# A hybrid encoder trunk on one core: the last product and its norm in two parts of 256 tokens, and another order of the sums and scalings ahead of the MLP

## The chip, the cores and the metric

The kernel runs on one core of a Trainium2 chip. The metric is the device time of one execution in microseconds; the median of three runs is given.

The engines are named as in the profile: PE is TensorE (PEld its weight loads), DVE is VectorE, ACT is ScalarE, POOL is GpSimd, SP is SyncE, which here only issues transfers. Each engine works through its own queue in the order in which the program issued the instructions to it; an instruction whose operand is not there holds up everything behind it in that queue.

## The reference, cut to what matters

One layer of an encoder on 1024 tokens of 1024 channels, all float32. Four token mixers make `merged`; then

```python
x = x + g1 * (merged @ w_out)
h2 = rmsnorm(x, norm2_g) * (1.0 + sc2) + sh2
f = square(relu(h2 @ w_ff1)) @ w_ff2          # D_FF = 4096
x = x + g2 * f
return rmsnorm(x, final_g)
```

with `rmsnorm(x, g) = x * rsqrt(mean(x*x over channels) + eps) * g`. The change touches only these lines: the second norm, the MLP's sums of weights, and the last product with the final norm.

## The kernel before

**Layout.** Tokens lie along the free dimension, channels on the partitions. `xg[k][t]` holds x for one half k of the channel blocks (even or odd) and one half t of the tokens (512 each): four slices m of 128 channels by 512 tokens. `xb(k, t, m)` is one slice.

**Precision.** A float32 product is made of three fp32r products: each operand is split into a high part (`whi`, `xhi`: a ScalarE copy) and a low part (`wlo`, `xlo`: VectorE subtracts), and TensorE adds up hi·hi, hi·lo and lo·hi.

**Stages and granules.** The second half of the program (`phase2`) is a list of 128 granules. Stage 0 is the product with `w_out` (granules 0 to 15). Stages 1 to 8 are the MLP: `w_ff1` and `w_ff2` in four blocks, each product by a scheme of seven instead of eight smaller products, so each stage has seven positions of two granules (h = 0, 1). Stage s begins at granule 16 + 14(s-1). The scheme needs sums of quarter matrices first: S1 to S4 of the weights, T1 to T4 of the other operand, all made by VectorE in pieces of 128x1024 (`wr<-wr,wr` in the profile for the weights). A granule is 24 matmuls of 512 columns (two halves p, four banks m, three products c), about 5.4 us. The two granules of a position fill four PSUM banks; the positions alternate between two sets of banks (`pm` and `pb` in the profile). `take` (or `take_out` in stage 0) reads a finished set: VectorE adds it into x, and where a norm follows, `square` squares x on ScalarE and VectorE adds the squares into `acc[t]`.

**The order by hand.** Iteration G of the loop issues, in this order: the taking of the last set, the matmuls of granule G with the functions of `at[(G, "mid")]` between their halves and those of `at[(G, "end")]` behind them, loads of weights, sums of weights (`w2_add`) for the granules ahead, sums of the other operand (`x2_add`), the weight split of granule G + 3 (`w2_split`), operand splits (`x2_split`), more loads. `w2_add(J)` makes the sums that granule J needs, as far as their forms are loaded and no form that is still to be split would be overwritten; what is missing is tried again later. It looks up to G + 4, and up to G + 8 for 8 <= G < 20.

**The norms.** `columns(t, bank)` adds the last squares, transposes `acc[t]` by TensorE in four blocks, reduces, takes the inverse root and makes `diag`, a diagonal block matrix; `spread(bank)` multiplies it with ones, so that every partition has the row, and ScalarE copies it to `rb`. `normed` then scales (VectorE) and shifts (ScalarE) x for the MLP; `final` scales x by the final gain and `rb` on VectorE and stores each slice of 256 KB, by SP and ACT in turn. For t = 1 the second norm's columns stand in the middle of granule 17, its spread in the middle of 18, and `normed` at the end of 18. The final norm of t = 0 has its columns in the middle of granule 125, its spread in the middle of 126, its scalings at the ends of 126 and 127. Behind the loop the last set (k = 0, t = 1) is taken, and t = 1 is normed and stored.

Of the kernel before, what the change touches and what calls it, by code (L numbers as in the profile page):

```python
# [6 lines left out]
F32 = mybir.dt.float32  # L7
F32R = mybir.dt.float32r
I32 = mybir.dt.int32
ACTF = mybir.ActivationFunctionType  # L10
ALU = mybir.AluOpType
# [33 lines left out]
class Program:  # L45
# [1502 lines left out]
    def phase2(self):  # L1548
        I, const, work = self.I, self.const, self.work
        md = {}  # L1550
# [14 lines left out]
        xg = self.xg = [[tile(f"xg{k}{t}", [128, 4, 512]) for t in range(2)] for k in range(2)]  # L1565
# [8 lines left out]
        xout = self.out.rearrange("(m k) p (t n) -> k t p m n", k=2, t=2)  # L1574
        for k, t in ((0, 0), (1, 0), (1, 1), (0, 1)):
            self.G.dma_start(out=xg[k][t], in_=xin[k, t])
        banks = [[self.mps() for _ in range(4)], [self.bps() for _ in range(4)]]
        xb = lambda k, t, m: xg[k][t][:, m, :]
        fb = lambda k, t, m: self.fr[k][t][m // 2][:, m % 2, :]
        ub = lambda m: self.u[m // 2][:, m % 2, :]  # L1580
        acc = [self.nrm[0][:, t, :] for t in range(2)]
        sqs = [self.nrm[1][:, t, :] for t in range(2)]
        diag, rb = (self.nrm[2][:, t, :] for t in range(2))
        begun = set()
# [6 lines left out]
        def take_out(i):  # L1591

            k, t = ((0, 0), (1, 0), (1, 1), (0, 1))[i]
            for m in range(4):
                upd(0, k, t, m, banks[i % 2][m])
                square(t, k, m)
            self.G.dma_start(out=xsp[k][t], in_=xg[k][t].rearrange("p c n -> p (c n)"))
# [51 lines left out]


        nsq, late = [0], []
        def square(t, k, m):

            if t not in begun:
                begun.add(t)
                self.act(acc[t], xb(k, t, m), ACTF.Square)
                return
            sq = sqs[nsq[0] % 2]
            nsq[0] += 1
            self.act(sq, xb(k, t, m), ACTF.Square)  # L1660
            squares()
            late.append((acc[t], sq))

        def squares():
            while late:
                a, sq = late.pop()
                self.add(a, a, sq)

        def columns(t, bank):

            squares()
            ss = self.sm.tile([128, 4], F32, tag="ss", name=self.name("ss"))
            for b in range(4):
                self.tr(bank[:, b * 128:(b + 1) * 128], acc[t][:, b * 128:(b + 1) * 128])
            self.reduce(ss, bank.rearrange("p (b c) -> p b c", c=128))
            r = self.drain(self.gen_rsqrt(ss, D))
            self.tt(diag.rearrange("p (b q) -> p b q", q=128), self.ident.unsqueeze(1).to_broadcast([128, 4, 128]),
                    r.unsqueeze(2).to_broadcast([128, 4, 128]), ALU.mult)
            begun.discard(t)

        def spread(bank):
            self.mm(bank, self.ones, diag)
            self.act(rb, bank, ACTF.Copy)

        def normed(k, t, h):
            for m in (2 * h, 2 * h + 1):
                d, x = 2 * m + k, xb(k, t, m)
                self.stt(x, x, A2[:, d:d + 1], rb, ALU.mult, ALU.mult)
                self.act(x, x, ACTF.Identity, bias=B2[:, d:d + 1])

        def final(k, t, h):
            for m in (2 * h, 2 * h + 1):
                d, x = 2 * m + k, xb(k, t, m)
                self.stt(x, x, self.col("fg", d), rb, ALU.mult, ALU.mult)
                self.dma(xout[k, t][:, m, :], x, "SA"[m % 2])

        at = {}
        on = lambda G, place, f: at.setdefault((G, place), []).append(f)
# [3 lines left out]
            on(10 + h, "end", lambda h=h: (normed(0, 0, h), normed(1, 0, h)))  # L1702
        on(17, "mid", lambda: columns(1, banks[1][0]))
        on(18, "mid", lambda: spread(banks[0][0]))
        for h in range(2):
            on(18, "end", lambda h=h: (normed(1, 1, h), self.x2_split(20 + h)))
        for h in range(2):
            on(18, "end", lambda h=h: (normed(0, 1, h), self.x2_add(22 + h)))
        on(27, "end", lambda: [self.dma(xg[k][t].rearrange("p c n -> p (c n)"), xsp[k][t]) for k, t in ((0, 0), (1, 1), (1, 0), (0, 1))])
        e = self.first(8)  # L1710
        on(e + 11, "mid", lambda: columns(0, banks[1][0]))
        on(e + 12, "mid", lambda: spread(banks[0][0]))
        for h in range(2):
            on(e + 12 + h, "end", lambda h=h: (final(0, 0, h), final(1, 0, h)))


        n_g = len(self.gran)
        for G in range(-4, n_g):
            if G >= 0:
                s, pos, h = self.gran[G]  # L1720
                if s == 0:
                    if G and G % 4 == 0:
                        take_out(G // 4 - 1)
                    bank, begins, ends, skip = banks[G // 4 % 2], G % 4 == 0, G % 4 == 3, False
                else:
                    n, (kind, order) = 7 * (s - 1) + pos, self.STAGES[s]
                    if h == 0:
                        take(n - 1) if n else take_out(3)
                    i, bank = order[pos], banks[n % 2]
                    skip = pos > 1 and order[pos - 2] == self.GOES_ON[kind].get(i)  # L1730
                    begins, ends = h == 0 and not skip, h == 1
                (whi, wlo), (xhi, xlo) = self.wops[G % 4], self.xop[G % 4]
                for p in range(2):
                    if p:
                        for f in at.get((G, "mid"), ()):
                            f()
                    for m in range(4):
                        o = slice(p * 512 + m * 128, p * 512 + (m + 1) * 128)
                        for c, (w, x) in enumerate(((whi, xhi), (whi, xlo), (wlo, xhi))):
                            self.mm(bank[m], w[:, o], x[:, p, :], start=begins and p == c == 0,  # L1740
                                    stop=ends and p == 1 and c == 2, skip=skip)
                for f in at.get((G, "end"), ()):
                    f()
            self.w2_loads(G + 8)
            for J in range(G + 1, min(G + (9 if 8 <= G < 20 else 5), n_g)):
                if 0 <= J:
                    self.w2_add(J)
            for J in range(G + 1, min(G + 5, n_g)):
                if J >= 0 and self.x2_own(J) and not 20 <= J < 24 and self.x2_there(J) <= G:
                    self.x2_add(J)  # L1750
            if G >= -3:
                self.w2_split(G + 3)
            for J in range(G + 1, min(G + 4, n_g)):
                if J >= 0 and self.x2_own(J) and (not 20 <= J < 24 or G >= 19) and self.x2_there(J) <= G:
                    self.x2_split(J)
            if G >= -3:
                self.x2_load(G + 3)
            self.w2_loads(G + 8)
        take(7 * 7 + 6)
        columns(1, banks[0][1])  # L1760
        spread(banks[0][2])
        for h in range(2):
            final(1, 1, h)
            final(0, 1, h)


def pack(inp):
# [67 lines left out]
```

## Time and profile before

| | |
|---|---|
| median of three runs | 1682.4 us (1679.68 to 1684.09) |
| profiled execution | 1681.92 us, span 1680.1 us, mean granted TensorE clock 0.991 |
| TensorE matmul busy | 1630.0 us (97%) |
| VectorE busy | 1259.2 us (75%) |
| ScalarE busy | 664.8 us (40%) |
| GpSimd busy | 64.9 us (4%) |

The span runs from the first to the last instruction of the profiled execution; the time of that execution is 1.8 us longer. Busy times are sums over the whole span, and matmul records overlap, so a busy TensorE is not one at its peak. Where an instruction waited, its row says in brackets how long its engine was idle ahead of it and which instruction ended that.

### The profile page before, as it was taken

The numbers are of one execution on the slowest core, as the hardware profiler recorded it, in microseconds if no ns is written. First come the engines' busy times: TensorE is split into PE (matmuls) and PEld (weight loads), VectorE is DVE, ScalarE is ACT, GpSimd is POOL, SyncE is SP. The second block draws the span as 40 slices with busy tenths as digits, with TensorE's granted clock in tenths as the row PEclk, the third lists the DMA queues.
The fourth block names the chain that finished last, engine by engine and source line by source line (L and its number), as shares of the span: only waits on it lengthen the run. The fifth ranks groups of instructions, "written<-read, shape, count | busy, mean of one in ns | idle before, by whom it ended". The sixth has DMA issues, their size and how long they took to land.

```text
span 1680.1 us, 19346 instructions
## 1 busy us (share of the span) xinstructions
PE 1630.0 (97%) x7390; PEld 1341.3 (80%) x7390; DVE 1259.2 (75%) x1906; ACT 664.8 (40%) x864; POOL 64.9 (4%) x126
## 2 busy tenths in 40 slices
PE   6999999999999999999999999899999999999995
PEld 4888878888878888888888888687888888888883
DVE  8889787779877865455666658899549947984897
ACT  5433323554336536541221335643243334323442
POOL 0000000000000000000000001100110010012000
PEclk9999999999999999999999999999999999999997
DMA  8522425533545453054564725661671274157102
GB/s 314 177 84 65 133 103 151 177 137 114 165 142 194 164 175 137 26 188 150 188 238 163 274 81 195 225 231 46 211 272 31 100 251 177 44 175 262 58 1 100
DMA packets 83679, 257.03 MB, mean 153 GB/s; under 512 B 9857, under 2 KB 22273, under 8 KB 82562
## 3 DMA queue, kind: packets, MB, share of 16 engines
q1 hardware_dynamic: 61186, 174.00, 30.6%
q0 software_dynamic: 17792, 67.12, 10.8%
q10 hardware_dynamic: 4608, 14.68, 2.2%
q8 instruction: 58, 0.95, 0.2%
q14 instruction: 35, 0.29, 0.1%
HBM read 199.14 MB, written 54.53 MB: 151 GB/s over the span
## 4 chain that ended last, share of the span: by engine, by line
PE 79%; DVE 14%; issue 2%; DMA 2%; ACT 2%; SPq 0%; DVEq 0%; ACTq 0%
PE pm L91 56%; PE pb L91 22%; DVE xg L122 2%; DVE wlo L105 2%; DVE xlo L105 1%; DVE fr L105 1%; DVE wr L105 1%; DVE t L105 1%; DVE s L126 1%; DVE fr L122 1%; DMA ada<-ada 1%; DVE nrm L105 1%; PE pb L96 1%; DVE ssacc L105 0%; DVE v L105 0%
## 5 line engine op out<-in xcount | busy, mean ns | idle before, releaser
L91 PE MATMUL pm<-act,whi 128*128 128x512 f32 x2176 | 672.9, 391 | 1.8 <-ACT act L146 1.6
L91 PEld LDWEIGHTS pm<-act,whi 128*128 128x128 f32 x2176 | 405.6, 188 | 88.3 <-ACT act L146 3.6
L91 PE MATMUL pm<-act,wlo 128*128 128x512 f32 x1088 | 419.8, 389 | 0.0
L146 ACT ACTIVATE whi<-wr 128x1024 fp32r<-128x1024 f32 x124 | 130.9, 1057 | 313.7 <-PE pm L91 133.0
L91 PEld LDWEIGHTS pm<-act,wlo 128*128 128x128 f32 x1088 | 204.3, 188 | 42.8
L105 DVE TENSOR_TENSOR wlo<-wr,whi 128x1024 fp32r<-128x1024 f32 x124 | 151.3, 1221 | 113.3 <-ACT whi L146 113.3
L91 PE MATMUL pm<-xhi,whi 128*128 128x512 f32 x512 | 201.0, 393 | 4.2 <-ACT whi L146 4.2
L91 PE MATMUL pb<-xhi,whi 128*128 128x512 f32 x512 | 201.0, 393 | 2.4 <-DVE xg L122 2.3
L91 PE MATMUL pm<-xhi,wlo 128*128 128x512 f32 x512 | 200.4, 391 | 2.0 <-DVE wlo L105 2.0
L91 PE MATMUL pm<-xlo,whi 128*128 128x512 f32 x512 | 200.1, 391 | 0.0
L91 PE MATMUL pb<-xhi,wlo 128*128 128x512 f32 x512 | 199.8, 390 | 0.0
L91 PE MATMUL pb<-xlo,whi 128*128 128x512 f32 x512 | 199.8, 390 | 0.0
L146 ACT ACTIVATE whi<-wraw 128x1024 fp32r<-128x1024 f32 x74 | 78.1, 1057 | 104.1 <-PE pm L91 87.4
L91 PEld LDWEIGHTS pm<-xhi,whi 128*128 128x128 f32 x512 | 96.7, 189 | 24.8 <-ACT whi L146 4.6
L91 PEld LDWEIGHTS pb<-xhi,whi 128*128 128x128 f32 x512 | 96.4, 188 | 24.1 <-ACT whi L146 2.7
L91 PEld LDWEIGHTS pm<-xhi,wlo 128*128 128x128 f32 x512 | 96.7, 189 | 22.6 <-DVE wlo L105 2.4
L91 PEld LDWEIGHTS pm<-xlo,whi 128*128 128x128 f32 x512 | 96.7, 189 | 20.5 <-DVE xlo L105 0.3
L91 PEld LDWEIGHTS pb<-xlo,whi 128*128 128x128 f32 x512 | 96.6, 189 | 20.3 <-issue 0.5
L91 PEld LDWEIGHTS pb<-xhi,wlo 128*128 128x128 f32 x512 | 96.5, 189 | 20.2
L105 DVE TENSOR_TENSOR wlo<-wraw,whi 128x1024 fp32r<-128x1024 f32 x74 | 90.1, 1219 | 8.0 <-ACT whi L146 7.7
L105 DVE TENSOR_TENSOR wr<-wr,wr 128x1024 f32<-128x1024 f32 x64 | 78.0, 1221 | 0.8
L105 DVE TENSOR_TENSOR xlo<-fr,xhi 128x1024 fp32r<-128x1024 f32 x54 | 65.9, 1220 | 11.7 <-ACT xhi L146 11.7
(263 smaller groups left out, 1879.8 us busy)
## 6 DMA issues: line engine op xcount, KB each, us to landing
wr<-w SPq DMA_DIRECT2D x76, 512.0 KB, 4.7
ada<-ada SPq DMA_DIRECT2D x48, 512.0 KB, 6.3
xhi<-hop POOLq DMA_DIRECT2D x42, 512.0 KB, 3.6
xlo<-hop POOLq DMA_DIRECT2D x42, 512.0 KB, 4.7
wraw<-wgate SPq DMA_DIRECT2D x32, 512.0 KB, 3.9
tg<-tg ACTq DMA_DIRECT2D x24, 512.0 KB, 2.8
tl<-tg SPq DMA_DIRECT2D x24, 512.0 KB, 5.6
wraw<-win SPq DMA_DIRECT2D x20, 512.0 KB, 3.6
```

Source lines behind the costliest of these rows:

```text
L91: self.P.matmul(out=out, lhsT=lhsT, rhs=rhs, start=start, stop=stop, skip_group_check=skip)
L96: self.P.transpose(out, a, self.ident)
L105: self.V.tensor_tensor(out=out, in0=a, in1=b, op=op)
L122: self.V.scalar_tensor_tensor(out=out, in0=a, scalar=s, in1=b, op0=op0, op1=op1, **kw)
L126: self.V.tensor_tensor_scan(out=out, data0=a, data1=b, initial=0.0, op0=ALU.mult, op1=ALU.add)
L146: self.A.activation(out=out, in_=a, func=f, **kw)
```

## The change

- The look-ahead of `w2_add` is split in two for all G: sums for granules up to G + 4 where they stood, and sums for G + 5 to G + 8 at the end of the iteration, behind the splits.
- The block at the end of granule 18 is issued in another order: both halves of `normed(1, 1)` first, then an operand split, one half of `normed(0, 1)`, another split, the other half, and the sums of granules 22 and 23 last.
- The loop ends at granule 125. The last product (granules 126 and 127) is made in two parts of 256 tokens, one after the other, each of 48 matmuls of 256 columns; the first part goes to the low halves of one set of banks, the second to the other set. The first part is taken while the second is multiplied, and its columns stand ahead of the second part's last 12 matmuls.
- Each part has its own columns and spread of 256 tokens. `last` scales a slice of 256 tokens by the final gain and directly by the spread bank, without a copy to `rb`, and stores it (128 KB) by SP or ACT. Between the two spreads stand two products of ones whose results are not used.
- For t = 0 the gain is multiplied in on ScalarE (`scaled`, eight copies with a scale at the end of granule 125) and `rb` on GpSimd (`final`, four products of 128x1024), stored in four transfers of 512 KB by SP.

```diff
-        def square(t, k, m):
+        def square(t, k, m, cut=slice(0, 512)):
+            a, x = acc[t][:, cut], xb(k, t, m)[:, cut]
...
-        def columns(t, bank):
+        def columns(t, bank, cut=slice(0, 512)):
             squares()
-            for b in range(4):
-                self.tr(bank[:, b * 128:(b + 1) * 128], acc[t][:, b * 128:(b + 1) * 128])
-            self.reduce(ss, bank.rearrange("p (b c) -> p b c", c=128))
+            a, d, nb = acc[t][:, cut], diag[:, cut], (cut.stop - cut.start) // 128
+            for b in range(nb):
+                self.tr(bank[:, b * 128:(b + 1) * 128], a[:, b * 128:(b + 1) * 128])
+            self.reduce(ss, bank[:, 0:128 * nb].rearrange("p (b c) -> p b c", c=128))
...
+        def spread(bank, cut=None):
+            if cut is None:
+                self.mm(bank, self.ones, diag)
+                self.act(rb, bank, ACTF.Copy)
+            else:
+                self.mm(bank[:, 0:cut.stop - cut.start], self.ones, diag[:, cut])
...
-        def final(k, t, h):
-            for m in (2 * h, 2 * h + 1):
-                d, x = 2 * m + k, xb(k, t, m)
-                self.stt(x, x, self.col("fg", d), rb, ALU.mult, ALU.mult)
-                self.dma(xout[k, t][:, m, :], x, "SA"[m % 2])
+        def scaled(k, t):
+            for m in range(4):
+                self.act(xb(k, t, m), xb(k, t, m), ACTF.Copy, scale=self.col("fg", 2 * m + k))
+
+        def final(k, t):
+            for h in range(2):
+                x = xg[k][t][:, 2 * h:2 * h + 2, :]
+                self.G.tensor_tensor(out=x, in0=x, in1=rb.unsqueeze(1).to_broadcast([128, 2, 512]), op=ALU.mult)
+                self.dma(xout[k, t][:, 2 * h:2 * h + 2, :], x)
+
+        def last(k, m, bank, cut):
+            x, d = xb(k, 1, m)[:, cut], 2 * m + k
+            self.stt(x, x, self.col("fg", d), bank[:, 0:cut.stop - cut.start], ALU.mult, ALU.mult)
+            self.dma(xout[k, 1][:, m, cut], x, "SA"[m % 2])
...
-        for h in range(2):
-            on(18, "end", lambda h=h: (normed(1, 1, h), self.x2_split(20 + h)))
-        for h in range(2):
-            on(18, "end", lambda h=h: (normed(0, 1, h), self.x2_add(22 + h)))
+        on(18, "end", lambda: (normed(1, 1, 0), normed(1, 1, 1), self.x2_split(20), normed(0, 1, 0), self.x2_split(21),
+                               normed(0, 1, 1), self.x2_add(22), self.x2_add(23)))
...
-        for h in range(2):
-            on(e + 12 + h, "end", lambda h=h: (final(0, 0, h), final(1, 0, h)))
+        on(e + 11, "end", lambda: (scaled(1, 0), scaled(0, 0)))
...
-        for G in range(-4, n_g):
+        for G in range(-4, n_g - 2):
...
-            for J in range(G + 1, min(G + (9 if 8 <= G < 20 else 5), n_g)):
-                if 0 <= J:
-                    self.w2_add(J)
+            for J in range(max(G + 1, 0), min(G + 5, n_g)):
+                self.w2_add(J)
...
             self.w2_loads(G + 8)
-        take(7 * 7 + 6)
-        columns(1, banks[0][1])
-        spread(banks[0][2])
-        for h in range(2):
-            final(1, 1, h)
-            final(0, 1, h)
+            for J in range(max(G + 5, 0), min(G + 9, n_g)):
+                self.w2_add(J)
+
+        take(7 * 7 + 5)
+        cuts = (slice(0, 256), slice(256, 512))
+        low, high = slice(0, 256), slice(256, 512)
+
+        def take_part(q):
+            for m in range(4):
+                x, d = xb(0, 1, m)[:, cuts[q]], 2 * m
+                self.stt(x, banks[1 - q][m][:, low], md["g2"][:, d:d + 1], x, ALU.mult, ALU.add)
+                square(1, 0, m, cuts[q])
+
+        def finals(q, bank):
+            for m in range(4):
+                for k in range(2):
+                    yield last(k, m, bank, cuts[q])
+
+        for q in range(2):
+            for h in range(2):
+                (whi, wlo), (xhi, xlo) = (o[(n_g - 2 + h) % 4] for o in (self.wops, self.xop))
+                for p in range(2):
+                    if (q, h, p) == (1, 1, 1):
+                        columns(1, banks[1][2][:, high], cuts[0])
+                    for m in range(4):
+                        o = slice(p * 512 + m * 128, p * 512 + (m + 1) * 128)
+                        for c, (w, x) in enumerate(((whi, xhi), (whi, xlo), (wlo, xhi))):
+                            self.mm(banks[1 - q][m][:, low], w[:, o], x[:, p, cuts[q]], start=h == p == c == 0,
+                                    stop=h == p == 1 and c == 2)
+                    if (q, h, p) == (0, 0, 0):
+                        spread(banks[0][0])
+                        final(1, 0)
+                        final(0, 0)
+            take_part(q)
+        spread(banks[1][3][:, high], cuts[0])
+        for _ in range(2):
+            self.mm(banks[1][0], self.ones, acc[0])
+        first, second = finals(0, banks[1][3][:, high]), finals(1, banks[0][1][:, high])
+        for _ in range(3):
+            next(first)
+        columns(1, banks[0][0][:, high], cuts[1])
+        spread(banks[0][1][:, high], cuts[1])
+        for _ in first:
+            pass
+        for _ in second:
+            pass
```

## Rows read from the trace of the kernel before

**Rows 1.** The page's first line.
```profile
span 1680.1 us, 19346 instructions
```

**Rows 2.** Windows: us from:to, length, busy PE, PEld, DVE, ACT, POOL, clock, DMA.
```profile
1012.00:1038.00 26.00, 26.00 (x116) 21.35 (x114) 25.58 (x30) 13.73 (x17) 4.79 (x10) 1.00 0.62 243
...
1058.00:1066.00 8.00, 1.86 (x8) 0.92 (x6) 7.14 (x8) 4.22 (x5) 0.53 (x1) 0.88 0.04 18
1066.00:1138.00 72.00, 72.00 (x307) 59.19 (x308) 68.39 (x76) 36.57 (x45) 7.94 (x15) 0.97 0.65 241
...
1146.00:1576.00 430.00, 429.87 (x1895) 355.37 (x1895) 313.98 (x338) 153.85 (x178) 44.07 (x84) 1.00 0.46 158
```

**Rows 3.** Chain that ended last: start us, us, engine, output, line, count.
```profile
1064.57 1.23 DVE wlo L105
1065.84 7.60 PE pm L91 x22
1073.45 10.88 PE pb L91 x48
...
1141.17 12.77 PE pb L91 x48
```

**Rows 4.** Timeline of PE: start us, us; in brackets idle before and its releaser.
```profile
249.60 0.61 PE L91 MATMUL pb<-v,ca 128*128 128x128 f32 x4
250.05 0.39 PE L91 MATMUL pb<-u,intra 128*128 128x128 f32 x2
...
1038.35 0.66 PE L96 MATMUL pb<-ident,nrm 128*128 128x128 f32 x4 [0.17 <-DVE nrm L105]
...
1141.17 0.47 PE L91 MATMUL pb<-xhi,whi 128*128 128x512 f32 x1 [2.31 <-DVE xg L122]
...
1657.84 0.39 PE L91 MATMUL pb<-xhi,wlo 128*128 128x512 f32 x1
```

**Rows 5.** Timeline of DVE, granules 12 to 18.
```profile
1015.99 2.47 DVE L105 TENSOR_TENSOR wr<-wr,wr 128x1024 f32<-128x1024 f32 x2
...
1033.06 2.36 DVE L105 TENSOR_TENSOR wr<-wr,wr 128x1024 f32<-128x1024 f32 x2
...
1037.60 0.69 DVE L105 TENSOR_TENSOR nrm<-nrm,nrm 128x512 f32<-128x512 f32 x1
...
1041.83 3.61 DVE L105 TENSOR_TENSOR wr<-wr,wr 128x1024 f32<-128x1024 f32 x3
...
1046.49 1.41 DVE L122 SCALAR_TENSOR_TENSOR xg<-xg,A,nrm 128x512 f32<-128x512 f32 x2
```

**Rows 6.** Timeline of ACT: high weight parts, and rb copied from its bank.
```profile
1016.11 1.99 ACT L146 ACTIVATE whi<-wr 128x1024 fp32r<-128x1024 f32 x2
...
1033.18 1.05 ACT L146 ACTIVATE whi<-wr 128x1024 fp32r<-128x1024 f32 x1
...
1045.36 0.60 ACT L146 ACTIVATE nrm<-pm 128x512 f32<-128x512 f32 x1 [2.29 <-PE pm L91]
...
1652.44 0.58 ACT L146 ACTIVATE nrm<-pm 128x512 f32<-128x512 f32 x1
```

**Rows 7.** Timeline of DVE, the block behind granule 18 and granule 32's taking.
```profile
1049.79 1.23 DVE L105 TENSOR_TENSOR xlo<-xg,xhi 128x1024 fp32r<-128x1024 f32 x1 [1.89 <-ACT xhi L146]
...
1057.57 1.23 DVE L105 TENSOR_TENSOR xg<-xg,xg 128x1024 f32<-128x1024 f32 x1 [0.79 <-ACT xg L146]
...
1140.28 2.72 DVE L122 SCALAR_TENSOR_TENSOR xg<-pb,g,xg 128x512 f32<-128x512 f32 x4
```

**Rows 8.** Timeline of DVE behind the last matmul.
```profile
1658.36 0.75 DVE L122 SCALAR_TENSOR_TENSOR xg<-pb,g,xg 128x512 f32<-128x512 f32 x1
...
1665.54 0.69 DVE L130 TENSOR_REDUCE ss<-pm 128x4 f32<-128x512 f32 x1 [1.21 <-PE pm L96]
...
1667.71 0.69 DVE L105 TENSOR_TENSOR nrm<-ident,rsq 128x512 f32<-128x512 f32 x1
...
1671.20 5.39 DVE L122 SCALAR_TENSOR_TENSOR xg<-xg,cols,nrm 128x512 f32<-128x512 f32 x8 [2.80 <-ACT nrm L146]
```

**Rows 9.** Groups by line and shape, DVE: count, busy us, mean ns, idle before.
```profile
L105 DVE TENSOR_TENSOR tt<-tt,t 128x256 f32<-128x256 f32 x16 | 6.1, 422 | 0.3
```

More of the change, by code (lines that the diff above doesn't have):

```diff
@@ L1651, in phase2 @@
         nsq, late = [0], []
-        def square(t, k, m):
+        def square(t, k, m, cut=slice(0, 512)):
+            a, x = acc[t][:, cut], xb(k, t, m)[:, cut]
             if t not in begun:
                 begun.add(t)
-                self.act(acc[t], xb(k, t, m), ACTF.Square)
+                self.act(a, x, ACTF.Square)
                 return
-            sq = sqs[nsq[0] % 2]
+            sq = sqs[nsq[0] % 2][:, cut]
             nsq[0] += 1
-            self.act(sq, xb(k, t, m), ACTF.Square)
+            self.act(sq, x, ACTF.Square)
             squares()
-            late.append((acc[t], sq))
+            late.append((a, sq))
         def squares():
@@ L1667, in squares @@
                 self.add(a, a, sq)
-        def columns(t, bank):
+        def columns(t, bank, cut=slice(0, 512)):
             squares()
-            ss = self.sm.tile([128, 4], F32, tag="ss", name=self.name("ss"))
-            for b in range(4):
-                self.tr(bank[:, b * 128:(b + 1) * 128], acc[t][:, b * 128:(b + 1) * 128])
-            self.reduce(ss, bank.rearrange("p (b c) -> p b c", c=128))
-            r = self.drain(self.gen_rsqrt(ss, D))
[L1677 to L1683, printed above, removed]
+            a, d, nb = acc[t][:, cut], diag[:, cut], (cut.stop - cut.start) // 128
+            ss = self.sm.tile([128, 4], F32, tag="ss", name=self.name("ss"))[:, 0:nb]
+            for b in range(nb):
+                self.tr(bank[:, b * 128:(b + 1) * 128], a[:, b * 128:(b + 1) * 128])
+            self.reduce(ss, bank[:, 0:128 * nb].rearrange("p (b c) -> p b c", c=128))
+            r = self.drain(self.gen_rsqrt(ss, D))
+            self.tt(d.rearrange("p (b q) -> p b q", q=128), self.ident.unsqueeze(1).to_broadcast([128, nb, 128]),
+                    r.unsqueeze(2).to_broadcast([128, nb, 128]), ALU.mult)
+            if cut.stop == 512:
+                begun.discard(t)
+        def spread(bank, cut=None):
[4 more added lines that the diff above has]
+                self.mm(bank[:, 0:cut.stop - cut.start], self.ones, diag[:, cut])
         def normed(k, t, h):
```

## The prediction, made before the changed kernel had run

> **What bounds the kernel now.** I read the windows first, for where each engine is full, then the chain that ended last, then the queues of TensorE, VectorE and ScalarE around the two places that the change touches. The span is 1680.1 us [rows 1]. From granule 34 on (1146 us) TensorE is full to the end of the products and VectorE has air: 429.9 of 430 us against 314 [rows 2]. So work moved between engines there costs and gives nothing; a gain must come from a place where TensorE waits. Three count; a short wait ahead of columns(0) in granule 125 keeps the same work ahead of it.
>
> At the start of stage 1 VectorE is the bound: 25.6 of 26 us busy up to 1038, 68.4 of 72 between 1066 and 1138 [rows 2]. TensorE pauses in granule 21 until 1065.84, when its low weight part has been split [rows 3], and again before granule 34, 2.31 us, because the bank that it is to write has not been taken [rows 4]. Behind the first pause the granted clock fell to the lower of its two levels, 1.2 GHz: 0.88 is the mean of that window [rows 2], and the 22 matmuls behind it took 7.60 us where 48 take 10.88, so 2.6 us more than at full clock. Behind the second, 48 took 12.77, 1.9 more [rows 3].
>
> The third place is the tail. The last matmul starts at 1657.84 and ends at 1658.2 [rows 4], and what follows runs in a line: taking the bank and adding squares from 1658.36, transposes, the reduction at 1665.54, root and diagonal at 1667.71, the spread, eight scalings from 1671.20 to 1676.59, and 3.5 us for the last transfer and the closing wait [rows 8].
>
> **The order of the weight sums.** The three sums S2, S4, S3 of granule 21 take 3.5 us on VectorE from 1041.83, and the split behind them 1.1 more, up to the first scaling at 1046.49; today they are issued in iteration 17, behind the norm's columns, so they fill the time in which diag goes through TensorE and comes back as rb [rows 5, 6]. By the new rule the sums of granule J+5 and beyond stand at the end of an iteration. S4 overwrites a form that iteration 16 has split by then, so all three are issued at the end of iteration 16: ahead of columns(1), not behind it. Following the queue:
>
> In iteration 12 the split of granule 15 now stands ahead of S1 and S2 of granule 20. VectorE is free at 1015.99, the high part ends at 1016.11 + 1.04, so VectorE idles 1.15 us where it had a sum to do [rows 5, 6]; some 0.3 of small gaps further on take that up: +0.9. In iteration 16 the split of granule 19 follows the bank's taking (which ends at 1033.06) at once, and its high part, at 1033.18, needs 1.05: +1.2 [rows 5, 6]. The last add of squares, at 1037.60 today, so starts 3.5 + 0.9 + 1.2 = 5.6 later. TensorE, which waits 0.17 ahead of the transposes today [rows 4], waits 5.6 more.
>
> From the transposes to the end of the copy of rb it is 1038.35 to 1045.96, 7.6 us, of which TensorE's 24 matmuls and the spread are most [rows 4, 6]. VectorE has the diagonal ready 3.5 us after the transposes start, at 1041.83, and then only the split of granule 20, 1.1 us. It idles 7.6 - 3.5 - 1.1 = 3.0 us.
>
> The new order of the norm gives some back. Four scalings now run in one go, and the waits for ScalarE fall from two of 1.9 and two of 0.8 us to two of 1.9 [rows 7]: with an overlap at the end I take 1.7 off. Sum on VectorE up to the split of granule 21, today at 1064.57 [rows 3]: 0.9 + 1.2 + 3.0 - 1.7 = +3.4 us. From there VectorE runs full to the taking at 1140.28 [rows 7], which lets granule 34 start, and the six sums of granules 32 to 35 stand ahead of it in either order, so nothing is won back on that way; TensorE's time is set by VectorE again.
>
> To this comes the clock. The new pause of 5.6 us is nearly as long as TensorE's idle 6.1 us in the window from 1058 to 1066, in which it fell [rows 2]. The 24 matmuls and the spread behind the transposes are on the path, and at the lower level they lose between nothing and the 2.6 us measured there. I take 2.2. **Stage 1: +5.6 us, between +3.4 and +6.0.** The sums of the later stages move four granules ahead inside iterations where TensorE never waits; their loads stand granules ahead of them, and VectorE has 116 us of air there: nothing.
>
> **The last product in two parts.** 96 matmuls of 256 columns replace 48 of 512, which take 10.88 us [rows 3]. The trace has none of that width. Below, half of 0.227 us, and no loss; above, the full 0.227 us each, 10.9 us more, if something fixed set the pace. The nearest row is four records of 128 columns, each with a weight load of its own, that start within 0.45 us, counted to the next row [rows 4]: a load fits in 0.113 us, so I take 0.12 and +0.6 us. Two pauses come in: the spread writes a bank that is being taken (0.4), and the second part's first bank is the one that ScalarE copies rb from, a copy that ends at 1653.0 today [rows 6] and about 0.6 later behind the eight new copies with a scale (half of the 1.04 us for 1024 elements each) [rows 6]. TensorE ends 1.6 us later, at 1659.8.
>
> On VectorE a 256-wide add is 0.42 us alone [rows 9], about 0.34 one behind another, and 0.40 with a PSUM source (half of the eight in 5.39 us [rows 8], with the fixed part). The eight scalings of the other token half leave it for GpSimd; they ran while TensorE was busy, so their going is worth only that the first part's taking finds VectorE free. Its transposes stand 12 matmuls ahead of TensorE's end, at 1658.2; 0.5 us to the reduction, 1.9 from there to the diagonal (2.17 today [rows 8] less the shorter reduction) and 0.4 for it make 1661.0, when VectorE can start on part two: 2.6 us of taking and adds, 1.2 for three scalings, 0.4 for the last add, and 0.5, 1.9 and 0.4 again: 1668.0. Five scalings cover the spread, at either clock, and eight follow it, 5.2 us in all: 1673.2. With the same 3.5 us behind it the span ends at 1676.7. **Tail: -3.4 us, between -1.5 (scalings that cost more, 16 transfers of 128 KB at half the pace) and -5 (no pauses).** The two extra products of ones lie in a wait of TensorE. ScalarE issues some of the transfers, each behind its scaling; the second root stands behind one that is done by then.
>
> GpSimd's four products of 1024 elements are not in the trace, where it only issues transfers. Below, VectorE's price of some 1.2 us [rows 5]; above, 4.3 us, where four of them from 1653.6 and a transfer would reach 1673. In between they are hidden, and so are SP's four transfers of them, ahead of the scalings' own in SP's queue.
>
> **Sum.** The profiled run took 1681.92 us: 1681.9 + 5.6 - 3.4 = 1684.1. The median shown is 0.5 above that run, so 1684.6 for the median.
>
> **Rivals.** *GpSimd stands in VectorE's way (slower), 0.35.* The four products run from 1653.6, just when VectorE adds the first part's squares, each add reading two SBUF tensors. If an add waits until the product under way has ended, four adds wait for four products: done at 1653.8 + 4 x (1.2 + 0.4) = 1660.2 in place of 1653.6 + 2.6 + 0.4 = 1656.6, and past 1658.2 the transposes ahead of TensorE's last 12 matmuls wait. At 1.2 us for a product that is +2.0 us, 1686.6; at twice that +6.8, 1691.4; past 1687.4 it goes from 1.4 us on. The rows speak neither for nor against: nothing in the trace has both engines computing. The Trainium skill (SBUF — State Buffer, Who interferes with whom) states just this rule: a Vector instruction with two SBUF inputs contends with a GpSimd one that reads SBUF, and whichever comes second is blocked for the whole instruction. Its GPSIMD Engine Reference (Performance versus the Vector engine) has 4497 ns for an add of 2048 elements, so by estimate 2.25 us here, and the sum by that is 1691. No run here shows it yet.
>
> *The order of the sums does no harm (faster), 0.18.* If the columns don't slip, only the norm's 1.7 us and the tail remain: 1681.9 - 1.7 - 3.4 + 0.5 = 1677.3, or 1679.0 without the 1.7. Against: VectorE had no gap of 3.5 us ahead of 1037.60.
>
> *The tail gives nothing, 0.10.* Were the small scalings and transfers so dear that they eat the 3.4 us, +5.6 remains: 1688. For it: VectorE's rows of 256 and 512 elements are 0.42 and 0.69 us, far from halving [rows 8, 9].
>
> **How the numbers follow.** My own case has 0.37, between 1680.8 (+3.4 and -5, with the 0.5) and 1687 (+6.0 and -1.5). A difference under 0.3%, 5 us, can't be told from none here: 1677.4 to 1687.4 is no change. My case is inside but for 0.03 below and 0.02 above, for what it has mispriced; the first rival is outside with 0.28 of 0.35, the second faster with 0.12 of 0.18 (it ends at the border, and the tail's -5 carries it past), the third slower with 0.07 of 0.10. Faster 0.15, same 0.48, slower 0.37. For 8 in 10 the range goes from 1677, the second rival's end, to 1691.5, the first's.
>
> **What would show it.** Right: the add of squares before columns(1) some 5 us later than 1037.60, a pause of 5 us in TensorE in granule 17, rb about 5 us later with VectorE idle ahead of it, granule 34 some 4 to 6 us later; the tail behind the last matmul 5 us shorter, 17 us for 22. Wrong: no pause in granule 17; matmuls of 256 columns far from 0.12 us apart; adds of squares that wait or stretch while GpSimd multiplies.

## The result, and the profile after

The changed kernel takes **1693.3 us** (median of 6 runs, 1691.1 to 1696.6) where the kernel before takes 1682.2 (6 runs, the three of the table above among them): a ratio of 1.007, 95% interval 1.0056 to 1.0083, so **slower by 11.1 us**. The forecast was 1684.6 with a range from 1677 to 1691.5, and 1693.3 lies above it. The profiled run took 1691.1 us, with this span and these windows (columns as in [rows 2]):

```profile
span 1689.3 us, 19510 instructions
```
```profile
1036.00:1057.00 21.00, 15.45 (x60) 12.07 (x59) 12.97 (x20) 8.36 (x13) 1.30 (x3) 0.84 0.38 138
1057.00:1066.00 9.00, 8.73 (x38) 6.59 (x36) 7.22 (x9) 5.61 (x8) 1.90 (x4) 1.00 0.59 235
1066.00:1140.00 74.00, 67.83 (x279) 54.40 (x280) 65.97 (x75) 35.26 (x45) 8.48 (x16) 0.95 0.60 227
1145.00:1576.00 431.00, 431.00 (x1902) 356.66 (x1901) 317.42 (x341) 154.60 (x177) 44.07 (x84) 1.00 0.45 158
...
1665.50:1671.00 5.50, 0.00 (x0) 0.00 (x0) 5.38 (x5) 0.83 (x2) 4.67 (x2) 0.72 0.50 191
```

From 1145 to 1576 us TensorE is full, as before [rows 2]. Three stretches differ: 1036 to 1057, where TensorE has 15.45 of 21 us and a clock of 0.84; 1066 to 1140, where TensorE is no longer full and VectorE is less busy than before (65.97 of 74); and the tail, where for 5.5 us TensorE does nothing while VectorE and GpSimd are both busy.

The work ahead of this stage ends at another time in each run, so I measure from one event, the anchor: the taking of the first product's bank in iteration 4, at 961.38 us in the profile of before and 959.96 after. VectorE's timeline, the anchor of before and then after from the anchor to the taking in iteration 32:

```profile
961.38 2.11 DVE L122 SCALAR_TENSOR_TENSOR xg<-pm,g,xg 128x512 f32<-128x512 f32 x3 [1.31 <-PE pm L91]
```
```profile
959.96 2.11 DVE L122 SCALAR_TENSOR_TENSOR xg<-pm,g,xg 128x512 f32<-128x512 f32 x3 [1.31 <-PE pm L91]
...
1035.76 1.23 DVE L105 TENSOR_TENSOR wlo<-wr,whi 128x1024 fp32r<-128x1024 f32 x1 [1.11 <-ACT whi L146]
...
1038.04 3.61 DVE L105 TENSOR_TENSOR wr<-wr,wr 128x1024 f32<-128x1024 f32 x3
1041.57 0.68 DVE L105 TENSOR_TENSOR nrm<-nrm,nrm 128x512 f32<-128x512 f32 x1
...
1052.03 2.74 DVE L122 SCALAR_TENSOR_TENSOR xg<-xg,A,nrm 128x512 f32<-128x512 f32 x4 [4.57 <-ACT nrm L146]
...
1116.57 1.23 DVE L105 TENSOR_TENSOR wr<-wr,wr 128x1024 f32<-128x1024 f32 x1 [4.61 <-DMA wr<-w]
1117.71 1.28 DVE L105 TENSOR_TENSOR fr<-fr,pb 128x512 f32<-128x512 f32 x2
...
1147.98 2.72 DVE L122 SCALAR_TENSOR_TENSOR xg<-pb,g,xg 128x512 f32<-128x512 f32 x4
```

The first four rows behind after's anchor are the forecast's: the split waits 1.11 us for its high part, the three sums of granule 21 stand ahead of the add of squares (in [rows 5] they stand behind it, at 1041.83), and VectorE then idles 4.57 us for rb. The next was not foreseen: one weight sum of granule 35 waits 4.61 us for its load, with a bank's taking queued behind it. SP's queue shows why that load is late, and the chain that ended last what it took:

```profile
1097.10 3.24 SPq L149 DMA_DIRECT2D xg<-xsp  x4
1100.39 6.24 SPq L149 DMA_DIRECT2D wr<-w  x4
```
```profile
1042.31 1.12 PE pb L96 x4
1043.42 4.36 PE pm L91 x12
1047.78 2.72 PE pb L91 x12
...
1098.21 1.15 DVE sp L122
...
1099.37 0.32 SPq L149
...
1100.39 16.16 DMA wr<-w
...
1650.18 4.34 PE pm L91 x12
```

The load stands in SP's queue behind four reloads of xg, 1 MB each, which wait for VectorE (the last two for the `sp` row of the chain, which ends at 1099.36). Issued at last, it lands beside those 4 MB and takes 16.2 us, where the median load of this kind on the page takes 4.0; from 1105 to 1117 us the 16 DMA engines are full, at 416 GB/s. The chain's first rows show the clock's part: behind TensorE's pause 12 matmuls take 4.36 us, the next 12 take 2.72, so 1.6 us are lost at the lower level (1.2 GHz). Its last row is the same loss once more, behind columns(0). TensorE's waits, in before ahead of columns(0) and then in after:

```profile
1643.03 0.66 PE L96 MATMUL pb<-ident,nrm 128*128 128x128 f32 x4 [1.51 <-DVE nrm L105]
```
```profile
1042.31 1.12 PE L96 MATMUL pb<-ident,nrm 128*128 128x128 f32 x4 [5.55 <-DVE nrm L105]
...
1143.45 0.50 PE L91 MATMUL pm<-xlo,whi 128*128 128x512 f32 x1 [1.47 <-DVE xlo L105]
...
1649.52 0.66 PE L96 MATMUL pb<-ident,nrm 128*128 128x128 f32 x4 [2.63 <-DVE nrm L105]
...
1671.04 0.69 PE L96 MATMUL pb<-ident,nrm 128*128 128x128 f32 x2 [5.59 <-DVE nrm L105]
```

The last is the tail's. VectorE and GpSimd there:

```profile
1660.49 2.45 DVE L105 TENSOR_TENSOR nrm<-nrm,nrm 128x512 f32<-128x512 f32 x1
1662.87 0.47 DVE L122 SCALAR_TENSOR_TENSOR xg<-pb,g,xg 128x256 f32<-128x256 f32 x1
1663.26 2.23 DVE L105 TENSOR_TENSOR nrm<-nrm,nrm 128x256 f32<-128x256 f32 x1
1665.41 0.47 DVE L122 SCALAR_TENSOR_TENSOR xg<-pb,g,xg 128x256 f32<-128x256 f32 x1
1665.81 2.17 DVE L105 TENSOR_TENSOR nrm<-nrm,nrm 128x256 f32<-128x256 f32 x1
```
```profile
1659.99 10.19 POOL L1705 TENSOR_TENSOR xg<-xg,nrm 128x1024 f32<-128x1024 f32 x4 [96.07 <-ACT nrm L146]
```

Beside GpSimd's products (2.55 us each on average) an add of 256 elements takes 2.2 us, where [rows 9] has 0.42; the takings between them, which read one operand in PSUM, keep their 0.47. Taken one by one, the four products end at 1662.40, 1665.20, 1667.69 and 1670.18, and the four adds 0.3 to 0.5 us behind them: each add ends only once the product under way has ended.

Measured from the anchor, in us (each distance is the difference of two starts in one profile; the end is the span's; the third is called the tail below):

| | before | after |
|---|---|---|
| to the taking in iteration 32 | 178.90 | 188.02 |
| to the transposes of columns(0) | 681.65 | 689.56 |
| from there to the end of the span | 37.07 | 39.78 |

So 7.9 us are lost up to columns(0) and 2.7 behind it, 10.6 together, where the medians have 11.1.

### The profile page after: what moved, and what is told of

It reads as the page before. It is cut to its first block, busy times and chain, and to the rows that moved or that the text cites. A ratio compares the mean times of both kernels' runs of the same rounds, so it can differ in the third digit from the quotient of the medians.

```text
span 1689.3 us, 19510 instructions
## 1 busy us (share of the span) xinstructions
PE 1636.3 (97%) x7444; PEld 1347.5 (80%) x7444; DVE 1263.4 (75%) x1922; ACT 669.7 (40%) x876; POOL 75.2 (4%) x130
## 4 chain that ended last, share of the span: by engine, by line
PE 78%; DVE 14%; DMA 3%; issue 2%; ACT 2%; SPq 1%; DVEq 0%; ACTq 0%
PE pm L91 56%; PE pb L91 21%; DVE wlo L105 2%; DVE xlo L105 1%; DVE xg L122 1%; DVE fr L105 1%; DVE nrm L105 1%; DMA wr<-w 1%; DVE wr L105 1%; SPq L149 1%; DMA ada<-ada 1%; DVE fr L122 1%; PE pb L96 1%; DVE t L105 1%; DVE s L126 1%
## 5 line engine op out<-in xcount | busy, mean ns | idle before, releaser
L91 PE MATMUL pm<-xhi,wlo 128*128 128x512 f32 (+1 forms) x528 | 206.3, 391 | 3.5 <-DVE wlo L105 3.5
L91 PE MATMUL pm<-xlo,whi 128*128 128x512 f32 (+1 forms) x528 | 206.5, 391 | 1.5 <-DVE xlo L105 1.5
L91 PE MATMUL pm<-xhi,whi 128*128 128x512 f32 (+1 forms) x528 | 207.3, 393 | 0.5 <-DVE fr L105 0.4
L91 PE MATMUL pb<-xhi,whi 128*128 128x512 f32 (+1 forms) x512 | 199.3, 389 | 2.5 <-DVE fr L105 2.5
L91 PE MATMUL pb<-xhi,wlo 128*128 128x512 f32 (+1 forms) x512 | 198.2, 387 | 0.0
L91 PE MATMUL pb<-xlo,whi 128*128 128x512 f32 (+1 forms) x512 | 198.1, 387 | 0.0
L91 PEld LDWEIGHTS pm<-xhi,wlo 128*128 128x128 f32 x528 | 101.0, 191 | 24.4 <-DVE wlo L105 3.9
L146 ACT ACTIVATE whi<-wraw 128x1024 fp32r<-128x1024 f32 x74 | 78.1, 1057 | 102.8 <-PE pm L91 86.1
L91 PEld LDWEIGHTS pm<-xlo,whi 128*128 128x128 f32 x528 | 100.8, 191 | 22.2 <-DVE xlo L105 1.9
L91 PEld LDWEIGHTS pm<-xhi,whi 128*128 128x128 f32 x528 | 100.9, 191 | 21.9 <-DVE fr L105 1.1
L146 ACT ACTIVATE xhi<-fr 128x1024 fp32r<-128x1024 f32 x54 | 56.6, 1049 | 52.7 <-DVE fr L122 32.9
```

What stands on the lines that cost most here:

```text
L91: self.P.matmul(out=out, lhsT=lhsT, rhs=rhs, start=start, stop=stop, skip_group_check=skip)
L146: self.A.activation(out=out, in_=a, func=f, **kw)
```

## The experiments

Each group below shared its runs of the kernel before, whose median was 1681.0 to 1682.5 in all four.

**First group: one cause taken away at a time.**

e1 gives the weight sums before's order again:
```diff
-            for J in range(max(G + 1, 0), min(G + 5, n_g)):
-                self.w2_add(J)
+            for J in range(G + 1, min(G + (9 if 8 <= G < 20 else 5), n_g)):
+                if 0 <= J:
+                    self.w2_add(J)
...
-            for J in range(max(G + 5, 0), min(G + 9, n_g)):
-                self.w2_add(J)
```


> The changed kernel with the weight sums issued in the order of the kernel before; the new order of the norm and the tail in two parts stay. Theory 1 (the order of the sums makes the loss: VectorE idles for the high parts and for rb, TensorE pauses at a low clock, and one sum waits for a late load): up to the last product's start the changed kernel lost 9.5 us, and the new order of the norm gives some 1.7 us back by itself, so 1693.3 - 9.5 - 1.7 = 1682.1, between 1680.5 and 1684, with columns(1) waiting under 0.5 us again. Theory 2 (the tail makes most of it): no less than 1688.

Measured: 1682.1 us, ratio to before 1.0006 (0.9996 to 1.0015). The three distances of the table are 176.59, 679.27, 39.79: 10.3 us less than after up to columns(0), and 2.4 less than before. The order of the sums makes the loss ahead of the tail; the new order of the norm is a gain. The tail is as long as in after.

e2 keeps the new order except for granule 21:
```diff
             for J in range(max(G + 5, 0), min(G + 9, n_g)):
-                self.w2_add(J)
+                if J != 21:
+                    self.w2_add(J)
```


> Only the three sums of granule 21 go back behind columns(1); every other sum keeps the new order. Theory 1: VectorE has them to do while it waits for rb (3.0 us), and TensorE's pause ahead of columns(1) shrinks from 5.55 to some 2.1 us, so most of the 2.2 us of clock loss goes too: 1693.3 - 3.0 - 1 to 2 = 1688.3 to 1689.3. Rival (a load decides: VectorE runs into the late load of granule 35 anyway, and what was won is waited away there): 1692 to 1693.5, with VectorE's idle time ahead of that sum up from 4.61 us by what was won.

Measured: 1687.2 us, ratio 1.0040 (1.0027 to 1.0053). Distances 183.01, 684.56, 39.78: 5.0 us better than after, so the first theory, a little beyond its figure. The wait for the load stays, in VectorE's timeline of e2:
```profile
1112.66 1.22 DVE L105 TENSOR_TENSOR wr<-wr,wr 128x1024 f32<-128x1024 f32 x1 [4.36 <-DMA wr<-w]
```
It is not soaked up there, because the reloads ahead of the load wait for VectorE and come earlier by as much (132.4 us behind the anchor for 137.1).

e3 moves the reloads one place on in SP's queue:
```diff
-        on(27, "end", lambda: [self.dma(xg[k][t].rearrange("p c n -> p (c n)"), xsp[k][t]) for k, t in ((0, 0), (1, 1), (1, 0), (0, 1))])
+        on(28, "mid", lambda: [self.dma(xg[k][t].rearrange("p c n -> p (c n)"), xsp[k][t]) for k, t in ((0, 0), (1, 1), (1, 0), (0, 1))])
```


> The four reloads of xg (4 MB) stand in SP's queue one place later, behind the load of granule 35's weight form in place of ahead of it; nothing else is changed. Theory 1 (the load came late because it stood behind the reloads, which wait for VectorE, and shared the transfer with them: 16.2 us): VectorE's idle 4.61 us ahead of the sum of granule 35 goes, granule 34 starts some 4.2 us earlier: 1693.3 - 4.2 = 1689.1. Rival (its buffer came free no earlier, or the wait goes to the reloads' own users): 1692.5 to 1694.

Measured: 1687.6 us, ratio 1.0042 (1.0029 to 1.0055). Distances 182.91, 684.45, 39.80: 5.1 us better than after, some more than expected. The timelines of e3, SP's queue and then VectorE's sums of granules 34 and 35:
```profile
1072.10 18.29 SPq L149 DMA_DIRECT2D wr<-w  x4
1099.90 3.10 SPq L149 DMA_DIRECT2D xg<-xsp  x4
```
```profile
1113.53 2.35 DVE L105 TENSOR_TENSOR wr<-wr,wr 128x1024 f32<-128x1024 f32 x2
```
The load is issued with the ones ahead of it, before 1090.4, not behind the reloads, and the sum follows the one before it without idle time.

e4 leaves GpSimd's products out, so half of its output is not scaled by `rb`:
```diff
-                self.G.tensor_tensor(out=x, in0=x, in1=rb.unsqueeze(1).to_broadcast([128, 2, 512]), op=ALU.mult)
```


> GpSimd's four products are left out, so the token half 0 of the output lacks the factor rb; its transfers stay. Theory 1 (GpSimd's products, 2.55 us each, hold VectorE's adds of two SBUF tensors): the adds of 256 elements take 0.42 us in place of 2.2 to 2.45, the first part's transposes no longer hold TensorE for 5.6 us, and the tail comes out 3.4 us shorter than before's in place of 1.1 longer: 1693.3 - 4.5 = 1688.8, between 1687.5 and 1690. Rival (the adds are long for another reason, or the path runs elsewhere): 1692.5 to 1693.5.

Measured: 1686.4 us, ratio 1.0032 (1.0019 to 1.0044). Distances 187.91, 689.44, 32.85: the tail is 6.9 us shorter than in after and 4.2 shorter than in before. That is more than the 4.5 expected. In after's profile 12 matmuls behind columns(0) ran at the lower level and lost 1.6 us (4.34 us for 2.7), which I had left out of the tail's account; e1 to e3 don't lose them there, and their tails are as long as after's all the same: TensorE spends some 0.7 us more in short gaps on the way and waits 0.9 longer for the adds (6.5 us for 5.6). So in all four runs VectorE's held adds set the tail's length, not TensorE's clock. e4 doesn't lose them either. The timelines of e4, VectorE and then TensorE:
```profile
1662.08 0.41 DVE L105 TENSOR_TENSOR nrm<-nrm,nrm 128x256 f32<-128x256 f32 x1
```
```profile
1667.98 2.42 PE L91 MATMUL pb<-nrm,ones 128*128 128x256 f32 x6 [0.97 <-DVE nrm L105]
```
The adds take 0.41 us again, and of TensorE's 5.6 us ahead of the first part's transposes nothing is left (the next wait is 0.97, for the diagonal).

**Second group: the norm alone, and the tail mended.** e5 is the kernel before with the lines of after for `on(18, "end", ...)`.

> The kernel before with only the new order of the norm behind granule 18. Theory: it alone takes two waits of VectorE for ScalarE away; e1, which has it and the new tail, stands 2.3 us ahead of before when granule 34's bank is taken, so this run should be 2.3 us below before, 1.6 to 2.8. Rival (TensorE's pauses soak it up): within 0.5 us of before.

Measured: 1679.7 us, ratio 0.9987 (0.9978 to 0.9995); distances 176.59, 679.23, 37.08: 2.3 us gained at the taking in iteration 32, kept to the end.

e6 replaces each product:
```diff
-                self.G.tensor_tensor(out=x, in0=x, in1=rb.unsqueeze(1).to_broadcast([128, 2, 512]), op=ALU.mult)
+                self.G.memset(x, 0.0)
```


> The changed kernel with each of GpSimd's four products replaced by a memset of the same tile, so token half 0 of the output is zero. Theory 1 (a GpSimd instruction that reads SBUF holds VectorE's adds of two SBUF tensors): a memset reads nothing, the adds of 256 elements take 0.42 us under it, and the time is e4's, 5 to 7 us below the changed kernel's. Rival (any GpSimd instruction on SBUF holds them): the adds stretch to the length of the memsets, and the gain shrinks by what they wait.

Measured: 1687.5 us, ratio 1.0033 (1.0020 to 1.0045). It tells nothing about the adds: a memset doesn't wait for rb, and the four ran from 1655.7 to 1660.3, ahead of them. e9 mends that. It tells something else: with nothing beside the adds, as in e4, but with the 1.6 us of clock lost behind columns(0) as in after (12 matmuls in 4.33 us), the tail is 33.73, 0.9 above e4's and 6.1 below after's.

e7 is e1 with the squares beside the products in PSUM (`set_[m]` is the bank just taken, `high` a free half):
```diff
-            sq = sqs[nsq[0] % 2][:, cut]
+            sq = sqs[nsq[0] % 2][:, cut] if sq is None else sq
...
-                        square(t, k, m)
+                        square(t, k, m, sq=set_[m] if i == 5 else None)
...
-                square(1, 0, m, cuts[q])
+                square(1, 0, m, cuts[q], None if q else banks[1][m % 2][:, high])
```


> e1 (weight sums as before), and the squares that VectorE adds while GpSimd multiplies are written to PSUM by ScalarE, so each of those adds reads one SBUF tensor and one in PSUM. Theory 1 (only two SBUF sources are held up): these adds take 0.4 to 0.75 us beside the products, and TensorE's 6.5 us wait ahead of the first part's transposes goes. But the small root operations and the diagonal of the first part, each with two SBUF sources, now come while the products still run, and may wait up to four times 2.5 us: between 1677 and 1681, against e1's 1682.1. Rival (VectorE is slowed by GpSimd whatever it reads): no change against e1.

Measured: 1680.1 us, ratio 0.9985 (0.9976 to 0.9994), tail 37.13. The timelines of e7, GpSimd's products and VectorE beside them:
```profile
1652.78 9.40 POOL L1705 TENSOR_TENSOR xg<-xg,nrm 128x1024 f32<-128x1024 f32 x4 [95.47 <-ACT nrm L146]
```
```profile
1652.45 0.68 DVE L105 TENSOR_TENSOR nrm<-nrm,pm 128x512 f32<-128x512 f32 x1
...
1653.44 0.41 DVE L105 TENSOR_TENSOR nrm<-nrm,pb 128x256 f32<-128x256 f32 x1
...
1658.04 1.87 DVE L118 TENSOR_SCALAR rsq<-ss 128x2 f32<-128x2 f32 x1
...
1660.38 2.02 DVE L105 TENSOR_TENSOR rsq<-rsq 128x2 f32<-128x2 f32 x2
```
With one operand in PSUM the adds keep their own time. The root's operations, of two elements each, are held in their place: 2.02 us for two that take 0.36 elsewhere, and also one with a single source, 1.87 for 0.17.

e8 is e7 and lets the products start earlier (`False` leaves out the transfers of `final`, and `scaled` here takes the slices to scale):
```diff
+        spread(banks[1][3])
+        final(1, 0)
+        final(0, 0, False)
         take(7 * 7 + 5)
...
-        on(e + 11, "end", lambda: (scaled(1, 0), scaled(0, 0)))
+        on(e + 11, "end", lambda: scaled(1, 0))
...
-                    if (q, h, p) == (0, 0, 0):
-                        spread(banks[0][0])
-                        final(1, 0)
-                        final(0, 0)
             take_part(q)
+            scaled(0, 0, (2 * q, 2 * q + 1))
+            self.dma(xout[0, 0][:, 2 * q:2 * q + 2, :], xg[0][0][:, 2 * q:2 * q + 2, :], "A")
```


> e7, and rb is spread and copied ahead of the last but one product's taking, so that GpSimd's products start some 4 us earlier and end by the first part's root; ScalarE's scaling of half 0, k = 0, moves behind its product. Theory: nothing with two SBUF sources is left beside the products, so the tail is e4's, 6.9 us shorter than e1's: 1675.5 to 1677, faster than both kernels. Rival (the spread's bank stops TensorE, or late transfers of 1 MB set the end): 1678 to 1682.

Measured: **1676.6 us**, ratio 0.9965 (0.9951 to 0.9978), tail 32.63. It leaves nothing out and is faster than both kernels. The timelines of e8, GpSimd and then VectorE:
```profile
1646.23 9.51 POOL L1705 TENSOR_TENSOR xg<-xg,nrm 128x1024 f32<-128x1024 f32 x4 [89.94 <-ACT nrm L146]
```
```profile
1652.09 0.41 DVE L105 TENSOR_TENSOR nrm<-nrm,pb 128x256 f32<-128x256 f32 x1
...
1656.29 0.17 DVE L118 TENSOR_SCALAR rsq<-ss 128x2 f32<-128x2 f32 x1
```
The products end at 1655.7, just ahead of the root. They take 2.38 us each here, and 2.55 in after, where the held adds alternate with them.

**Third group: what in GpSimd's instruction holds VectorE.** In e9 the product becomes
```diff
+                if k and not h:
+                    self.G.tensor_copy(out=md["g1"][:, 0:1], in_=rb[:, 0:1])
+                for _ in range(3):
+                    self.G.memset(x, 0.0)
```
and in e10 `self.G.tensor_copy(out=x, in_=rb.unsqueeze(1).to_broadcast([128, 2, 512]))`.

> The changed kernel with each of GpSimd's four products replaced by three memsets of the same tile (0.95 us each in e6), behind a copy of one column of rb, so that they run when the products ran, beside the adds of squares; token half 0 of the output is zero. Theory 1 (what holds VectorE's adds is GpSimd reading SBUF): memsets read nothing, the adds of 256 elements take 0.42 us beside them, and the time is e4's, 6 to 7 us below the changed kernel's. Rival (any GpSimd instruction that uses SBUF holds them): the adds take up to 1 us, four of them 2 us more in all, and the time lies 2 to 4 us above e4's.

> The changed kernel with each of GpSimd's four products replaced by a copy of rb into the same tile, which reads one SBUF tensor in place of two; token half 0 of the output is rb alone. Theory 1: one read is enough, each add of squares waits until the copy under way has ended and the time goes down only as far as a copy is shorter than 2.55 us. Rival (it takes two reads by GpSimd): the adds take 0.42 us and the time is e4's.

Measured: e9 1687.0 us, ratio 1.0037 (1.0026 to 1.0048), e10 1687.6, ratio 1.0037 (1.0022 to 1.0051). The timelines, first e9's GpSimd and VectorE, then e10's:
```profile
1661.44 11.73 POOL L1708 MEMSET xg<- 128x1024 f32 x12
```
```profile
1662.84 0.42 DVE L105 TENSOR_TENSOR nrm<-nrm,nrm 128x256 f32<-128x256 f32 x1
...
1667.52 0.73 DVE L118 TENSOR_SCALAR rsq<-ss 128x2 f32<-128x2 f32 x1
```
```profile
1661.76 4.85 POOL L1705 COPY xg<-nrm 128x1024 f32<-128x1024 f32 x4 [96.04 <-ACT nrm L146]
```
```profile
1663.66 0.86 DVE L105 TENSOR_TENSOR nrm<-nrm,nrm 128x256 f32<-128x256 f32 x1
```
Beside memsets the adds take 0.42 us; beside copies of 1.2 us, which read one tensor, 0.86. So one read by GpSimd is enough to hold an add of two SBUF tensors, and writing alone does nothing to it. The one-source operation is held by memsets too (0.73). As times, e9 and e10 lie too close to e4 to tell apart; the verdict rests on the rows. The tails agree with them: both runs lost the clock behind columns(0) as e6 did, and against its 33.73 e9 has 34.32, longer by about what the one-source operation was held, and e10 34.18.

**Fourth group: do the parts add up?** e11 is e2 and e3 together, e12 the kernel before with after's order of sums alone (e1's diff, the other way round).

> e2 and e3 together: the sums of granule 21 back behind columns(1), and the load of granule 35 ahead of the reloads. Theory: the two are separate losses of 5 to 6 us each, so the time is 1693.3 - 5.9 - 5.5 = 1681.9, up to 1.5 more where TensorE can't use all of it, and what is left of the new order (the idle 1.1 us for a high part, three times) costs 0 to 2 us against e1. Rival (one loss seen twice: what one gives back the other had already): 1686 to 1688.

> The kernel before with only the new order of the weight sums. Theory: the three parts of the change add up; the new order of the norm gives 2.7 us back (e5) and the tail costs 2.7 by e1's and before's profiles, so the order alone makes what is left, 11 us: 1691.5 to 1694. Rival (the sums' order hurts only together with four scalings in one go behind rb): 1686 to 1689.

Measured: e11 1683.3 us, ratio 1.0014 (1.0005 to 1.0023), distances 178.52, 680.08, 40.18; e12 1692.5 us, ratio 1.0071 (1.0057 to 1.0084), distances 189.67, 691.22, 37.10. The parts add. Against e1, e11 has 0.8 us more at columns(0), which is what else the order costs; its tail is 0.4 longer because its transposes behind columns(0) ran at the lower level (1.11 us for 0.65). In e12 the pauses of granule 17 and ahead of columns(0) are as in after, by TensorE's timeline:
```profile
1042.81 1.11 PE L96 MATMUL pb<-ident,nrm 128*128 128x128 f32 x4 [5.54 <-DVE nrm L105]
...
1651.70 0.66 PE L96 MATMUL pb<-ident,nrm 128*128 128x128 f32 x4 [2.62 <-DVE nrm L105]
```

## Why the prediction was wrong

The account, by distances, in us:

| part of the change | forecast | measured | from |
|---|---|---|---|
| order of the sums, granule 21's behind columns(1) | +3.0, and 2.2 of clock | +5.0 | after less e2 |
| order of the sums, load of granule 35 | 0 | +4.5 | e2 less e11 |
| order of the sums, the rest | +2.1 | +0.8 | e11 less e1 |
| new order of the norm | -1.7 | -2.4 | e1, e5 less before |
| tail in two parts | -3.4 | -4.2 | e4 less before |
| GpSimd in VectorE's way | 0 | +6.9 | after less e4 |
| sum | +2.2 | +10.6 | |

The last two parts are measured at e4's clock; where TensorE ran at the lower level behind columns(0), they are -3.3 and +6.1 (by before, e6 and after), with the same sum. Why after, e6, e9 and e10 lost the clock there and e1 to e4 didn't, no run tells.

**The step that failed** is the one that set the likeliest case: "GpSimd's four products of 1024 elements are not in the trace ... In between they are hidden". They are not; the first rival was right, with its place, its mechanism and its price. It gave +2.0 at 1.2 us for a product and +6.8 at twice that; a product takes 2.35 (e7's four in 9.40) to 2.55 us, and the price was 6.1 to 6.9. The prediction gave this 0.35 because "the rows speak neither for nor against". That was true of the rows, but the adds with two SBUF operands stood in the same microseconds as the products, and so nothing spoke for hiding either. The estimate of 2.25 us from the Trainium skill (GPSIMD Engine Reference, Performance versus the Vector engine) is a little under the 2.35 measured. The rule of the Trainium skill (SBUF — State Buffer, Who interferes with whom) held: whichever comes second is blocked for the whole of the other instruction. e9 and e10 agree with its finer part as well, that a GpSimd instruction that only writes doesn't hold two-source ones (0.42 us beside memsets, 0.86 beside copies). For one-source operations the same section of the Trainium skill says that they can contend when they run in a mode that uses both of VectorE's port pairs. The stretched ones of e7 (1.87 us) and e9 (0.73) are in line with that; whether they ran in such a mode, no row shows.

**The second miss is the range.** With the rival at its upper price the forecast was 1691.4, and 1693.3 lies above it, because of a wait that neither the case nor a rival held. The prediction followed the sums as work of VectorE ("the six sums of granules 32 to 35 stand ahead of it in either order, so nothing is won back") and that was right: six sums stand there in both. What a sum moved forward needs, its load, it asked only of the later stages ("their loads stand granules ahead of them"). In iteration 27 one load stands behind four reloads that wait for VectorE, and the sum came to it 4.6 us too early.

Point by point, the other steps:

- **Granule 21's sums ahead of columns(1): right.** The split's waits of 1.1 us in iterations 12 and 16, the add of squares 5.4 us later (1041.57 for 1037.60, and the run 1.42 earlier), TensorE's pause of 5.55 for 5.6, VectorE's idle time ahead of rb 4.57 for 3.0: the difference is the clock's 1.6 us, which arrives through VectorE's wait, where the forecast had the clock beside VectorE. The transposes took 0.5 more as well (1.12 us for 0.66), so from the transposes to rb the clock cost 2.1, for the 2.2 forecast. The split of granule 21 came 4.9 us later (1068.06 for 1064.57, and the 1.42), about the forecast of 3.4 and the 1.6 together.
- **"TensorE's time is set by VectorE again": right up to granule 34, too high beyond.** Without the load's wait, in e3, the taking comes 4.0 us later, as forecast ("some 4 to 6"). But of that 2.8 are left at columns(0), where 1.1 is a wait of its own. In before, TensorE lost 1.9 us of clock behind its pause at granule 34 [rows 3]; in after the last pause there is 1.47 us and the clock is 1.00 from 1145 on. The kernel had that loss to give back, most of the 2.3 us between 4.0 and 2.8 less 1.1, and the sum didn't credit it.
- **"The sums of the later stages ...: nothing": nearly.** Ahead of columns(0) the same thing happens as in granule 12: a sum that filled the wait for a high part has moved on, VectorE idles 1.11 us, and TensorE's wait is 2.63 us for 1.51. So "inside iterations where TensorE never waits" was wrong for this one, and so was "a short wait ahead of columns(0) in granule 125 keeps the same work ahead of it".
- **The norm's order: right, 1.7 forecast, 1.7 found with the new order of sums (after less e12), 2.4 without.**
- **The tail: right but for GpSimd.** -4.2 (-3.3 at the lower clock) for -3.4. Matmuls of 256 columns start 0.12 us apart in TensorE's timeline of after, as taken from the rows of 128 columns:
```profile
1656.77 0.28 PE L91 MATMUL pb<-xlo,whi 128*128 128x256 f32 x1
1656.89 0.28 PE L91 MATMUL pb<-xhi,wlo 128*128 128x256 f32 x1
```
- **The rivals "no harm" and "tail gives nothing": wrong**, by e1 and e12, and by e4.

One thing stays open: e2, e3 and e11 don't add to the tenth. The load's wait is worth 5.1 us with the pause of granule 17 and 4.5 without it; no run tells why.

## What to carry to other kernels

Before work goes to an engine that was idle, list what the other engines do in those microseconds and which operands they share with it: here the four products, 2.4 us each, cost 6 to 7 us, and nothing that the tail shows once the adds beside them read PSUM and the products ended ahead of the root (32.63 in e8, 32.85 without products in e4). Before an operation is moved forward, follow its inputs as well as its engine: for each load, what stands ahead of it in its queue and what those entries wait for. And a filler in a wait is worth as much as the wait: three sums that filled 3.0 us cost 5.0 when they were moved, for the pause brought the clock down too.

## What the runs showed of the hardware

Unexpected was how small an operation can be and still be held: two elements for each partition took 1.87 us in place of 0.17 beside a GpSimd product (e7), and 0.73 beside memsets (e9), with one source and no second SBUF operand. An add of 256 elements beside memsets kept its 0.42 us. And the transfer itself was a part of the late load's price: issued 0.05 us behind the last reload, it took 16.2 us; issued ahead of the reloads, it was never waited for (e3).
